# Three convolution slots, an attention bank for the value chunk, and conv loads a block ahead, in a hybrid encoder kernel

## The chip, the core and the metric

The kernel runs on one core of a Trainium2 chip. The core has five engines with instruction streams of their own: TensorE (PE, matmuls and transposes; its weight loads are listed as PEld), VectorE (DVE), ScalarE (ACT), GpSimd (POOL) and SyncE (SP). In this kernel SyncE does nothing but issue transfers between HBM and the core's memory, in the order of its stream: one that has to wait holds up those behind it. Matmuls write into banks of PSUM, all other tiles live in SBUF. The metric is device time in microseconds (us): 1510.81 is the median of three runs (1509.77 to 1511.25).

## What is computed

One encoder layer, applied to a prompt of 512 tokens and to a sample of 1024 tokens, with 1024 channels and in float32:

```python
h = _rmsnorm(x, norm_attn_g[l])
z = h @ w_in[l]            # q | k | v | ca | cb
a_out = _window_attn(q, k, v, bias, band, attn_sink[l])
c = ca * jax.nn.sigmoid(cb)
c = _dwconv(c, conv_dw_w[l], conv_dw_b[l])            # 31 taps
c = jax.nn.silu(_layernorm(c, conv_ln_g[l], conv_ln_b[l]))
x = x + jnp.concatenate([a_out, c], axis=-1) @ w_out[l]
h = _rmsnorm(x, norm_ffn_g[l])
u = _dwconv(h @ w_up[l], ffn_dw_w[l], ffn_dw_b[l])    # 3 taps
x = x + (jax.nn.silu(u[..., :D_FF]) * u[..., D_FF:]) @ w_down[l]
y = _rmsnorm(x, norm_final_g)
```

## The kernel before

**Products.** Every large product is made of three matmuls: both factors are split into a rounded part ("hi") and the rest ("lo"), and hi x hi, hi x lo and lo x hi are added in PSUM. So each chunk of weights is loaded raw, cast to its hi part by ScalarE (L225) and subtracted to its lo part by GpSimd or VectorE (L226). The three matmuls stand on lines 337, 338 and 340 for the projections, and on 761, 762 and 763 for the out-projection.

**Memory.** `Slots` (L70) hands out fixed slots of SBUF by class: 15 q slots of 4096 bytes, 4 c slots of 4224, 61 h slots of 2048, 2 d slots of 2176 and 32 small ones (L188). A tile takes the smallest class that fits, in the order in which slots were given back. A name like h14_260_1700 is slot h14, its 260th tile, the 1700th of the program. PSUM's eight banks are dealt out in the same way: three a, two u, two b and one c; the table `use` says which a job may take (L190). In the sample's pass the projections (job "step") may take b alone, the attention (job "attn") a or u.

**Stages.** 0 to 105 us: norm and projection of the prompt. 105 to 320: the projection of the sample by chunks of w_in, in two halves of 512 tokens (`step`, L483, which calls `evac`, L407, to take a finished chunk from its bank); beside it, as side work, the attention and out-projection of the prompt. 340 to 650: the up-projection of the prompt (`ffn_step`), with the attention of the sample beside it (`sample`). 650 to 755: the out-projection of the sample, block by block (the loop at L1141), with three kinds of side work: the right halves of w_out (`right_halves`), the layer norms of the convolution's blocks (`conv_norm`, L713) and eleven sums of pairs (`pair_sums`, L923). Behind that the up-products and down-products of the sample, with an order on PE that is written by hand.

**What the change touches.** In `evac`, the value chunk (the last branch, from L448 on) is copied from its bank by ScalarE (L450), transposed by four PE instructions into a second bank (L453), and split from there (L460, L461). `conv_norm(i)` loads block i of the convolution from DRAM (cvd, L719) and its half of the concatenation (L711), transposes it on PE (L725), normalises (L731 on VectorE), transposes back (L737) and applies the swish. `pair_sums(p)` loads 512 KB from DRAM (gt[p]) into a c slot g (L926), makes four sums on GpSimd into a second c slot r (L932 to L935) and stores r to gb[p] (L936). gt[p] was stored by the gated steps of the prompt (L921), the last one being gt10.

**What sets the order.** `tick` (L315) advances side work: after each group of matmuls a rate is added to `due`, and for each whole unit one step of a generator runs. All instructions then pass a scheduler, which orders each engine's stream by priorities and modelled times; slots and banks are bound to tiles in program order. A transfer into a slot waits until the slot's last reader is done, and where that reader is a store, until it has landed.

Of the kernel before, what the change touches and what calls it, by code (L numbers as in the profile page):

```python
# [15 lines left out]
P = 128  # L16
# [35 lines left out]
NE = 2  # L52
# [5 lines left out]
KEEP = 3  # L58
# [111 lines left out]
def tile_hybrid_encoder(ctx: ExitStack, tc: tile.TileContext, xs, rel_bias, norm_attn_g, w_in,  # L170
                        attn_sink, conv_dw_w, conv_dw_b, conv_ln_g, conv_ln_b, w_out, norm_ffn_g,
                        w_up, ffn_dw_w, ffn_dw_b, w_down, norm_final_g, onehot, outs):
    nc = tc.nc
# [9 lines left out]

    homes = dict(q=full, h=big, c=odd, d=odd, s=small)
    small.tile([P, FILL], F32, name="fill")
    for tag, n in (("d0", 576), ("d1", 576), ("c0", 1088), ("c1", 1088), ("c2", 1088), ("c3", 1088)):
        odd.tile([P, n], F32, tag=tag, name=f"{tag}_0", bufs=1)
    sb = Slots(lambda tag: homes[tag[0]], dict(q=(15, 4096), c=(4, 4224), h=(61, 2048), d=(2, 2176), s=(32, 64)), "q", KEEP)  # L188
    banks = Slots(lambda tag: ps[two_of[tag]], dict(a=(3, 2048), u=(2, 2048), b=(2, 2048), c=(1, 2048)))
    use = dict(step="aub", turn="aub", last="c", conv="c", attn="au", norm="b", out="b", up="u", down="b")  # L190

# [3 lines left out]
    def bank(job):  # L195
        return banks.tile([NT], among=use[job])
# [210 lines left out]
    def evac(kind, c, nt, src):  # L407
        g, n = (0, 0) if nt == 0 else (1, nt - 1)
        T = GR[g]["T"]
        cols = slice(n * NT, (n + 1) * NT)  # L410
        if kind == "cb":
            t = sb.tile([NT])
            nc.scalar.activation(t[:], src, AF.Tanh, scale=0.5)
            tanh_t[nt, c] = t
        elif kind == "ca":
            if n == 0:
                cp = sb.tile([T + 2 * PAD])
                nc.gpsimd.memset(cp[:, 0:PAD], 0.0)
                nc.gpsimd.memset(cp[:, PAD + T:2 * PAD + T], 0.0)
                cpads[g, c] = cp  # L420
            cp = cpads[g, c]
            nc.vector.scalar_tensor_tensor(cp[:, PAD + n * NT:PAD + (n + 1) * NT], tanh_t.pop((nt, c))[:], 1.0, src,
                                           op0=ALU.add, op1=ALU.mult)
        elif kind == "q":
            hi, lo = sb.tile([NT], F32R), sb.tile([NT], F32R)
            nc.scalar.activation(hi[:], src, AF.Identity, scale=QSCALE)
            nc.vector.scalar_tensor_tensor(lo[:], src, QSCALE, hi[:].bitcast(F32),
                                           op0=ALU.mult, op1=ALU.subtract)
            for e in range(2):
                for L, s in ((0, hi), (1, lo)):  # L430
                    nc.sync.dma_start(
                        qsd[nt][:, L * HD:(L + 1) * HD, 2 * c + e, :].rearrange("b p t -> p b t"),
                        s[e * HD:(e + 1) * HD, :].bitcast(F32).rearrange("p (b t) -> p b t", t=P))
        elif kind == "k":
            hi, lo = sb.tile([NT], F32R), sb.tile([NT], F32R)
            nc.scalar.copy(hi[:], src)
            nc.vector.tensor_tensor(lo[:], src, hi[:].bitcast(F32), op=ALU.subtract)
            for kv in range(NKV):
                if g == 0:
                    kt[0, kv] = [sb.tile([T], F32R) for _ in range(2)]  # L440
                for L, s in ((0, hi), (1, lo)):
                    src_k = s[kv * HD:(kv + 1) * HD, :].bitcast(F32)
                    if g == 0:
                        for half in range(2):
                            nc.sync.dma_start(kt[0, kv][L][half * HD:(half + 1) * HD, :].bitcast(F32), src_k)
                    else:
                        nc.sync.dma_start(ksd[:, kv, L, cols], src_k)
        else:  # L448
            vs = sb.tile([NT])
            nc.scalar.copy(vs[:], src)  # L450
            pt = bank("step")
            for i in range(4):
                nc.tensor.transpose(pt[:, i * P:(i + 1) * P], vs[:, i * P:(i + 1) * P], ident[:])  # L453
            src = pt[:].rearrange("p (b c) -> p b c", c=P)
            vs = []
            for kv in range(NKV):
                v = sb.tile([4, P], F32R)
                head = slice(kv * HD, (kv + 1) * HD)
                rest = slice((1 - kv) * HD, (2 - kv) * HD)
                nc.scalar.copy(v[:, :, head], src[:, :, head])  # L460
                nc.vector.tensor_tensor(v[:, :, rest], src[:, :, head], v[:, :, head].bitcast(F32), op=ALU.subtract)  # L461
                if g == 1:
                    nc.sync.dma_start(vsd[:, n, kv], v[:].bitcast(F32))
                vs.append(v)
            if g == 0:
                vt[0] = vs
# [241 lines left out]
    def load_cat(i):  # L708
        cats[i, 0] = (sb.tile([4, P], F32R), sb.tile([4, P], F32R))
        for L in range(2):  # L710
            nc.sync.dma_start(cats[i, 0][L][:].bitcast(F32), catd[blocks[i][1], :, L, :].rearrange("p (j t) -> p j t", t=P))  # L711

    def conv_norm(i):  # L713
        G, b = blocks[i]
        if G["g"] == 0:
            drain(convs)
        cat = cat_of(i, 1)
        cv = sb.tile([4, P])
        nc.sync.dma_start(cv[:], cvd[G["g"]][:, :, b * P:(b + 1) * P])  # L719
        if G["g"] == 1 and (i, 0) not in cats:  # L720
            load_cat(i)
        yield 0.0
        pt = bank("norm")
        for c in range(4):
            nc.tensor.transpose(pt[:, c * P:(c + 1) * P], cv[:, c, :], ident[:])  # L725
        st, mv, rs = sm(6), sm(2), sm(1)
        nc.vector.bn_stats(st[:], pt[:])
        nc.vector.bn_aggr(mv[:], st[:])
        rstd_of(mv[:, 1:2], 1.0, rs[:])
        xh = sb.tile([CCH])  # L730
        nc.vector.tensor_scalar(xh[:], pt[:], mv[:, 0:1], rs[:], op0=ALU.subtract, op1=ALU.mult)  # L731
        del pt
        for _ in range(YN):
            yield 0.0
        p2 = bank("norm")
        for c in range(4):
            nc.tensor.transpose(p2[:, c * P:(c + 1) * P], xh[:, c * P:(c + 1) * P], ident[:])  # L737
# [215 lines left out]
    def sample():  # L953
# [13 lines left out]
        drain(late)  # L967
        for m in range(NE):
            yield from conv_norm(4 + m)
        for kc in range(KC):  # L970
            load_wo(kc, 1)

# [164 lines left out]

    side.extend((right_halves(), conv_norm(4 + NE)))
    side.extend(pair_sums(p) for p in range(NPAIR))
    pace.update(rate=2.2)  # L1140
    for i in range(4, NB - 2):  # L1141
        if 4 < i < NB - NE:
            side.appendleft(conv_norm(i + NE))
        if i == 8:
# [569 lines left out]
```

## Time and profile before

| what | value |
|---|---|
| median of three runs | 1510.81 us |
| the profiled execution | 1509.34 us, span 1507.5 us |
| mean granted clock of PE | 0.997 |
| PE busy | 1484.8 us, 98% of the span |
| PE's waits in the first 110 us | 3.1 us (L274, L296, L337, L338) |
| PE's waits behind 750 us | 2.7 us (L1119 on ACT, L1121 on POOL, L1042 on DVE) |

In the page and the views, one row is one instruction or a group. "a<-h,h" says which kind of slot or bank is written from which. "[1.92 <-DMA h<-qsd]" is idle time of the engine ahead of the row, and what ended it. Matmuls overlap in the array, so that their listed time (0.39 us) is longer than the step from one start to the next. SPq rows are issues of transfers; when one landed is read from the engine that waited for it.

### The profile page before, as it was taken

To read this page: it belongs to the slowest core of one execution; us is meant where nothing else is said; L and a number is where in the kernel's file an instruction comes from. 1 tells how busy PE (TensorE), PEld (TensorE's weight loads), DVE (VectorE), ACT (ScalarE), POOL (GpSimd) and SP (SyncE) were. 2 spreads that over 40 slices of the span, in tenths; PEclk is the share of its full clock that TensorE was granted. 3 is DMA by queue.
4 is the path that set the end of the run, shared out by engine and by line. 5 is a ranking of instruction groups with operands and counts; after the bars stand their busy time and mean duration, and the time that the engine had idled before them with its cause. 6 is when DMAs were issued, how large, how long until landed. Compare 5 with 4: busy or idle time off the path is not lost. (4 is left out here: it accounts for less than half of the span.)

```text
span 1507.5 us, 20010 instructions
## 1 busy us (share of the span) xinstructions
PE 1484.8 (98%) x6857; PEld 1225.2 (81%) x6857; DVE 1125.6 (75%) x1612; ACT 801.9 (53%) x1417; POOL 686.6 (46%) x546
## 2 busy tenths in 40 slices
PE   9999999999999999999999999999999999999998
PEld 7888787888888888778877888888888888888886
DVE  4889888878698885756868777777776845568884
ACT  6635646435877777534355554454445633444254
POOL 6642435236766676665325554554554000003345
PEclk9999999999999999999999999999999999999999
DMA  7762335455444436796222333333331772356644
GB/s 231 219 194 69 105 98 147 140 175 177 145 133 126 134 123 200 247 343 227 89 71 92 100 100 100 105 105 106 105 119 64 235 266 84 109 171 222 218 165 168
DMA packets 222443, 227.16 MB, mean 151 GB/s; under 512 B 12564, under 2 KB 162012, under 8 KB 222213
## 3 DMA queue, kind: packets, MB, share of 16 engines
q1 hardware_dynamic: 222341, 225.88, 46.6%
q8 instruction: 54, 0.88, 0.2%
q14 instruction: 48, 0.39, 0.1%
HBM read 164.74 MB, written 62.14 MB: 150 GB/s over the span
## 5 line engine op out<-in xcount | busy, mean ns | idle before, releaser
L226 POOL TENSOR_TENSOR q<-q,q 128x1024 fp32r<-128x1024 f32 x72 | 174.2, 2423 | 100.4 <-ACT q L225 37.2
L995 POOL TENSOR_TENSOR q<-q,q 128x512 fp32r<-128x512 f32 x101 | 140.8, 1401 | 154.0 <-ACT q L1105 141.8
L995 DVE TENSOR_TENSOR h<-h,h 128x512 fp32r<-128x512 f32 (+2 forms) x202 | 154.5, 797 | 67.1 <-ACT h L999 26.6
L1461 PE MATMUL w<-h,h 128*128 128x512 f32 x462 | 179.7, 389 | 0.0
L1459 PE MATMUL w<-h,h 128*128 128x512 f32 x458 | 178.2, 389 | 0.0
L1460 PE MATMUL w<-h,h 128*128 128x512 f32 x458 | 178.2, 389 | 0.0
L1119 PE MATMUL w<-h,q 128*128 128x512 f32 x448 | 175.0, 391 | 1.4 <-ACT w L1199 1.4
L1121 PE MATMUL w<-h,q 128*128 128x512 f32 x448 | 174.4, 389 | 1.1 <-POOL q L995 1.1
L1120 PE MATMUL w<-h,q 128*128 128x512 f32 x426 | 165.8, 389 | 0.0
L337 PE MATMUL u<-h,q 128*128 128x512 f32 x384 | 153.3, 400 | 1.6 <-DVE h L889 1.2
L338 PE MATMUL u<-h,q 128*128 128x512 f32 x384 | 151.4, 394 | 0.3 <-DVE h L299 0.3
L340 PE MATMUL u<-h,q 128*128 128x512 f32 x368 | 144.3, 392 | 0.0
L392 DVE SCALAR_TENSOR_TENSOR c<-c,cvw,c 128x512 f32<-128x512 f32 x184 | 138.1, 751 | 2.6
L992 POOL TENSOR_TENSOR q<-q,q 128x1024 f32<-128x1024 f32 x12 | 32.7, 2738 | 230.7 <-DVE q L992 213.4
L999 ACT CAST h<-h 128x512 fp32r<-128x512 f32 x120 | 72.0, 620 | 92.1 <-DVE h L995 40.6
L225 ACT CAST q<-q 128x1024 fp32r<-128x1024 f32 (+1 forms) x73 | 75.8, 1044 | 60.4 <-POOL q L226 23.4
L337 PE MATMUL b<-h,q 128*128 128x512 f32 x264 | 105.3, 400 | 0.0
L338 PE MATMUL b<-h,q 128*128 128x512 f32 x264 | 104.5, 396 | 0.0
L340 PE MATMUL b<-h,q 128*128 128x512 f32 x264 | 104.1, 395 | 0.3 <-POOL q L226 0.3
L1461 PEld LDWEIGHTS w<-h,h 128*128 128x128 f32 x462 | 86.7, 188 | 18.0
L1459 PEld LDWEIGHTS w<-h,h 128*128 128x128 f32 x458 | 86.0, 188 | 18.0
L1119 PEld LDWEIGHTS w<-h,q 128*128 128x128 f32 x448 | 84.2, 188 | 20.1 <-ACT w L1199 2.6
(435 smaller groups left out, 3657.7 us busy)
## 6 DMA issues: line engine op xcount, KB each, us to landing
q<-in_w_up SPq DMA_DIRECT2D x88, 512.0 KB
ga<-q SPq DMA_DIRECT2D x64, 256.0 KB
h<-ga SPq DMA_DIRECT2D x57, 256.0 KB
q<-in_w_in SPq DMA_DIRECT2D x28, 512.0 KB
h<-in_w_down SPq DMA_DIRECT2D x52, 256.0 KB
q<-in_x_sample SPq DMA_DIRECT2D x15, 512.0 KB
x1d<-q SPq DMA_DIRECT2D x11, 512.0 KB
gt<-h SPq DMA_DIRECT2D x22, 256.0 KB
```

What stands on the lines that cost most here:

```text
L226: ins = (nc.vector if dve else nc.gpsimd).tensor_tensor(lo[:], raw[:], hi[:].bitcast(F32), op=ALU.subtract)
L337: nc.tensor.matmul(out, whi[:, kc, :], hi[:], start=(kc == 0), stop=False)
L338: nc.tensor.matmul(out, whi[:, kc, :], lo[:], start=False, stop=False)
L340: nc.tensor.matmul(out, wlo[:, kc, :], hi[:], start=False, stop=(kc == KC - 1))
L392: nc.vector.scalar_tensor_tensor(acc[:], src(t), w(t), acc[:], op0=ALU.mult, op1=ALU.add)
L995: (eng or nc.vector).tensor_tensor(out, a, b, op=ALU.subtract)
L1119: nc.tensor.matmul(out, whi[:, s], hi[:], start=(start and c == 0), stop=False, **go)
L1120: nc.tensor.matmul(out, whi[:, s], lo[:], start=False, stop=False, **go)
L1121: nc.tensor.matmul(out, wlo[:, s], hi[:], start=False, stop=(stop and c == 3), **go)
L1459: nc.tensor.matmul(out, sh[:, c], th[:], start=(p == 0), stop=False)
L1460: nc.tensor.matmul(out, sh[:, c], tl[:], start=False, stop=False)
L1461: nc.tensor.matmul(out, sl[:, c], th[:], start=False, stop=(p == NPAIR - 1))
```

## The change

It has four parts.

1. One c slot fewer and two h slots more (L186 to L188): 3 x 4224 + 63 x 2048 = 141,696 bytes in place of 4 x 4224 + 61 x 2048 = 141,824.
2. In the sample's pass the value chunk's transposes take a bank of the attention, a or u, and no longer one of the two b banks (L451).
3. The load of a convolution block is taken out of `conv_norm` into `load_conv`, and the loop over the blocks calls it a block ahead; the first such load is issued at the end of `sample`.
4. The rate of side work in the out-projection's first blocks is 1.5 in place of 2.2.

```diff
-    for tag, n in (("d0", 576), ("d1", 576), ("c0", 1088), ("c1", 1088), ("c2", 1088), ("c3", 1088)):
+    for tag, n in (("d0", 576), ("d1", 576), ("c0", 1088), ("c1", 1088), ("c2", 1088)):
...
-    sb = Slots(..., dict(q=(15, 4096), c=(4, 4224), h=(61, 2048), d=(2, 2176), s=(32, 64)), "q", KEEP)
+    sb = Slots(..., dict(q=(15, 4096), c=(3, 4224), h=(63, 2048), d=(2, 2176), s=(32, 64)), "q", KEEP)
...
-            pt = bank("step")
+            pt = bank("attn" if g else "step")
...
+    cvs = {}
+
+    def load_conv(i):
+        G, b = blocks[i]
+        cv = cvs[i] = sb.tile([4, P])
+        nc.sync.dma_start(cv[:], cvd[G["g"]][:, :, b * P:(b + 1) * P])
+        if G["g"] == 1 and (i, 0) not in cats:
+            load_cat(i)
+
     def conv_norm(i):
...
-        cv = sb.tile([4, P])
-        nc.sync.dma_start(cv[:], cvd[G["g"]][:, :, b * P:(b + 1) * P])
-        if G["g"] == 1 and (i, 0) not in cats:
-            load_cat(i)
-        yield 0.0
+        if i not in cvs:
+            load_conv(i)
+            yield 0.0
+        cv = cvs.pop(i)
...
             yield from conv_norm(4 + m)
+        load_conv(4 + NE)
...
-    pace.update(rate=2.2)
+    pace.update(rate=1.5)
     for i in range(4, NB - 2):
+        if i + NE + 1 < NB:
+            load_conv(i + NE + 1)
```

NE is 2 and NB is 12. The number of instructions is the same on every engine (PE 6858, DVE 1614, ACT 1275, SP 783, POOL 551); what moves is the order, and the slots and banks. Lines behind 710 are numbered 8 to 11 higher in the new program.

**First place: PE at the value chunk, about 153 to 160 us before.** L453 is the transposes of the value chunk, L666 and L610, L680 and L681 the prompt's attention, L337 to L340 the projection; h14_260 and h10_261 are queries loaded from DRAM. Before:

```order
L453 MATMUL b1_88_1686<-ident_91,h8_258_1684 128x128 [waits DVE_49,Activation_49]
L453 MATMUL b1_88_1686<-ident_91,h8_258_1684 128x128 x3
...
L681 MATMUL a2_85_1616<-q14_248_1598,h34_145_867 128x512 [waits DVE_49]
L680 MATMUL a2_85_1616<-q14_248_1598,h34_145_867 128x512
...
L610 MATMUL u0_102_1866<-h1_127_767,h14_260_1700 128x384 [waits DMAHW7_49,DVE_49]
L610 MATMUL u0_102_1866<-h2_128_768,h14_260_1700 128x384
L337 MATMUL b1_91_1713<-h4_130_781,q9_234_1493 128x512 [waits DVE_49,PE_49]
L338 MATMUL b1_91_1713<-h22_131_782,q9_234_1493 128x512
L340 MATMUL b1_91_1713<-h4_130_781,q1_235_1494 128x512
```

Now the transposes stand amid the projection into b1_91, in bank a0, and a cluster of attention comes later, ahead of the first lo matmul into b0_109:

```order
L337 MATMUL b1_91_1714<-h35_148_881,q4_235_1493 128x512
L453 MATMUL a0_88_1685<-ident_90,h18_258_1683 128x128 [waits Activation_49]
L453 MATMUL a0_88_1685<-ident_90,h18_258_1683 128x128 x3
L338 MATMUL b1_91_1714<-h31_149_882,q4_235_1493 128x512
...
L338 MATMUL b0_109_1948<-h38_84_553,q6_273_1798 128x512
L680 MATMUL u0_98_1795<-q0_205_1275,h33_146_869 128x512 [waits Activation_49]
L681 MATMUL u0_98_1795<-q7_269_1757,h33_146_869 128x512 [waits DVE_49]
...
L666 MATMUL u0_106_1917<-ident_90,h9_264_1707 128x128 [waits DVE_49,PE_49]
...
L680 MATMUL a1_108_1941<-q9_289_1916,h32_145_866 128x512 [waits Activation_49]
L340 MATMUL b0_109_1948<-h37_83_552,q10_274_1799 128x512 [waits Pool_49]
```

That L340 waits for POOL, where the subtraction that writes q10_274 (L226, from the raw chunk q3_253) now stands behind the one that writes q1_295 and behind an L692 of the attention, which waits for VectorE's L690 (h15_279). POOL now:

```order
L692 TENSOR_TENSOR q8_247_1591<-h15_257_1672,h16_256_1671 64x512 [waits DVE_49]
L645 TENSOR_SCALAR q11_266_1724<-q11_266_1724,s5_263_1703 128x384 [waits DVE_49,PE_49]
L226 TENSOR_TENSOR q1_295_1945<-q12_272_1796,q14_294_1944 128x1024 [waits DMAHW2_49,Activation_49]
L692 TENSOR_TENSOR q8_247_1591<-h15_279_1842,h16_278_1841 64x512 [waits DVE_49,Pool_49]
L226 TENSOR_TENSOR q10_274_1799<-q3_253_1640,q6_273_1798 128x1024 [waits DMAHW6_49,Pool_49]
```

Before, the same subtraction (it wrote q4_273 there) stood ahead of both.

**Second place: PE at the prompt's last scores, about 247 to 254 us before.** L666 transposes weights of the attention, L680 and L681 use the copies of these transposes; the last L340 takes a chunk's lo part. Before:

```order
L666 MATMUL u0_144_2606<-ident_91,h18_350_2394 128x128
L338 MATMUL b1_142_2579<-h56_155_910,q14_348_2375 128x512
...
L338 MATMUL b0_146_2653<-h38_84_554,q11_364_2509 128x512
L680 MATMUL a2_145_2614<-h8_374_2595,h35_146_870 128x512 [waits DVE_49,Activation_49]
L681 MATMUL a2_145_2614<-q3_375_2596,h35_146_870 128x512 [waits DVE_49]
L680 MATMUL a2_145_2614<-q3_375_2596,h35_146_870 128x512 [waits Activation_49]
L681 MATMUL a2_145_2614<-q4_376_2611,h35_146_870 128x512 [waits DVE_49]
L340 MATMUL b0_146_2653<-h37_83_553,q12_365_2510 128x512 [waits Pool_49]
```

Now (the last L666 into u0_143 stands 30 rows ahead of the L680 shown, and the last two scores, of q14_378, 25 rows behind it):

```order
L338 MATMUL b0_146_2655<-h38_84_553,q7_366_2510 128x512
L680 MATMUL a1_145_2615<-h18_376_2596,h33_146_869 128x512 [waits DVE_49,Activation_49]
L733 MATMUL u1_147_2682<-ident_90,h14_387_2674 128x128 x3
L681 MATMUL a1_145_2615<-h5_377_2597,h33_146_869 128x512 [waits DVE_49]
L340 MATMUL b0_146_2655<-h37_83_552,q2_367_2511 128x512 [waits Pool_49]
L337 MATMUL b0_146_2655<-h39_85_568,q7_366_2510 128x512
```

**Third place: SP in the out-projection, from about 650 us before.** gt is loaded into g, r is stored to gb; cvd and catd are loads for the layer norms. Before, a load takes c0 or c2, a store c1 or c3:

```order
L936 DMA gb3_3448<-c3_1090_6928 128x1024 [waits DMAHW3_49,Pool_49]
L926 DMA c2_1108_7030<-gt5_3439 128x1024 [waits DMAHW5_49]
L214 DMA q4_1161_7325<-in_x_sample 128x1024 [waits PE_49]
L921 DMA gt10_3444<-h33_1025_6582 128x512 [waits DMAHW6_49,Pool_49]
L719 DMA h0_1080_6880<-cvd1_168 128x4x128 [waits DMAHW7_49,PE_49]
L711 DMA h15_1081_6882<-catd_166 128x512 [waits DMAHW0_49,PE_49]
L936 DMA gb4_3449<-c1_1107_7009 128x1024 [waits DMAHW1_49,Pool_49]
L926 DMA c0_1110_7050<-gt6_3440 128x1024 [waits DMAHW2_49]
```

Now c0, c1 and c2 go round, and a load into a slot follows the store out of the same slot (gb2 out of c0, then gt4 into c0; gb3 out of c2, then gt5 into c2; gb4 out of c1, then gt6 into c1):

```order
L944 DMA gb2_3450<-c0_1110_7009 128x1024 [waits DMAHW3_49,Pool_49]
L711 DMA h5_1048_6699<-catd_165 128x512 [waits DMAHW4_49,DVE_49]
L214 DMA q5_1138_7179<-in_x_sample 128x1024 [waits PE_49]
L934 DMA c0_1128_7123<-gt4_3441 128x1024 [waits DMAHW3_49]
...
L944 DMA gb3_3451<-c2_1112_7036 128x1024 [waits DMAHW0_49,Pool_49]
...
L934 DMA c2_1130_7150<-gt5_3442 128x1024 [waits DMAHW6_49,DMAHW0_49]
L944 DMA gb4_3452<-c1_1129_7124 128x1024 [waits Pool_49]
...
L718 DMA h38_1097_6943<-cvd1_167 128x4x128 [waits DMAHW3_49,DVE_49]
L934 DMA c1_1174_7421<-gt6_3443 128x1024 [waits DMAHW7_49,DMAHW4_49]
L929 DMA gt10_3447<-h8_1045_6690 128x512 [waits DMAHW5_49,Pool_49]
```

The last row is the store of the last gated step; the cast that takes the slot h8 next (h8_1057, from a raw part of w_out's right half) comes behind it on ScalarE, and PE's first out-projection matmul with that cast behind the cast.

More of the change, by code (lines that the diff above doesn't have):

```diff
@@ L185, in tile_hybrid_encoder @@
     small.tile([P, FILL], F32, name="fill")
-    for tag, n in (("d0", 576), ("d1", 576), ("c0", 1088), ("c1", 1088), ("c2", 1088), ("c3", 1088)):
+    for tag, n in (("d0", 576), ("d1", 576), ("c0", 1088), ("c1", 1088), ("c2", 1088)):
         odd.tile([P, n], F32, tag=tag, name=f"{tag}_0", bufs=1)
-    sb = Slots(lambda tag: homes[tag[0]], dict(q=(15, 4096), c=(4, 4224), h=(61, 2048), d=(2, 2176), s=(32, 64)), "q", KEEP)
+    sb = Slots(lambda tag: homes[tag[0]], dict(q=(15, 4096), c=(3, 4224), h=(63, 2048), d=(2, 2176), s=(32, 64)), "q", KEEP)
     banks = Slots(lambda tag: ps[two_of[tag]], dict(a=(3, 2048), u=(2, 2048), b=(2, 2048), c=(1, 2048)))
```

## The prediction

> **What bounds the kernel now.** I read the page from the top, then the waits of TensorE, then stretches of time, then single rows. The page first (busy time, share of the span, instructions):
>
> ```profile
> span 1507.5 us, 20010 instructions
> ...
> PE 1484.8 (98%) x6857; PEld 1225.2 (81%) x6857; DVE 1125.6 (75%) x1612; ACT 801.9 (53%) x1417; POOL 686.6 (46%) x546
> ```
>
> TensorE (PE) is the bound, and its matmuls are not touched by the change: both programs have 6858 PE instructions. So the change can only win time in which PE waits, or runs below its clock, and can only lose time by new waits. The profiled execution took 1509.34 us, 1.84 more than its span and 1.47 below the median of 1510.81; I work out differences against it and apply them to the median.
>
> How much waiting is there? The view of PE's waits over the whole span (engine, line, written tile, what ended the wait, us, times, longest), the rows that bear on the change:
>
> ```profile
> PE u L610 <- DMA h<-qsd: 1.9, 1, 1.9
> ...
> PE u L337 <- DVE h L889: 1.2, 1, 1.2
> PE a L725 <- DMA h<-cvd: 1.1, 1, 1.1
> ...
> PE b L453 <- ACT h L450: 0.8, 1, 0.8
> ...
> PE c L761 <- DVE q L766: 0.6, 1, 0.6
> PE u L761 <- ACT h L225: 0.5, 1, 0.5
> ...
> PE a L737 <- DVE h L731: 0.4, 1, 0.4
> ```
>
> These seven come to 6.5 us, 0.4% of the time. The same in stretches (length, PE busy and count, weight loads, DVE, ACT, POOL, granted clock, DMA share, GB/s):
>
> ```profile
> 150.00:160.00 10.00, 6.69 (x38) 5.01 (x37) 9.00 (x21) 9.03 (x21) 2.02 (x2) 1.00 0.49 158
> 160.00:170.00 10.00, 10.00 (x44) 8.30 (x44) 7.31 (x17) 4.66 (x12) 4.65 (x4) 0.83 0.09 30
> ...
> 250.00:260.00 10.00, 8.54 (x34) 5.89 (x33) 7.17 (x8) 9.14 (x17) 8.94 (x5) 1.00 0.96 274
> ...
> 650.00:660.00 10.00, 9.77 (x44) 7.79 (x43) 4.56 (x6) 3.22 (x6) 7.61 (x11) 1.00 0.83 275
> 660.00:670.00 10.00, 8.33 (x38) 6.32 (x37) 4.26 (x7) 0.62 (x1) 6.23 (x8) 1.00 1.06 388
> 670.00:680.00 10.00, 9.17 (x42) 6.93 (x41) 4.39 (x9) 2.76 (x6) 7.39 (x13) 1.00 1.06 395
> ```
>
> Three places lose time where the change moves rows: the value chunk of the sample's projection (150 to 165 us), the prompt attention beside it (250 to 256), and the sample's out-projection (650 to 680). Behind 760 us the order on PE is the same in both programs, so I count that part at nothing.
>
> **The value chunk (line 451).** PE's timeline (start, us, what it is, and in brackets the idle time before it):
>
> ```profile
> 145.05 0.39 PE L337 MATMUL b<-h,q 128*128 128x512 f32 x1
> ...
> 156.04 0.50 PE L681 MATMUL a<-q,h 128*128 128x512 f32 x1 [0.60 <-DVE q L669]
> ...
> 159.75 0.59 PE L610 MATMUL u<-h,h 128*128 128x384 f32 x2 [1.92 <-DMA h<-qsd]
> ...
> 161.09 0.61 PE L338 MATMUL b<-h,q 128*128 128x512 f32 x1
> ...
> 164.49 0.41 PE L337 MATMUL b<-h,q 128*128 128x512 f32 x1
> 164.74 0.39 PE L338 MATMUL b<-h,q 128*128 128x512 f32 x1
> 164.97 0.39 PE L340 MATMUL b<-h,q 128*128 128x512 f32 x1
> ```
>
> Matmuls of 512 columns start 0.23 us apart (164.74, 164.97), whatever their listed length. The waits of this place are 0.8 (L453) + 0.6 + 1.9 = 3.3 us. Behind them eight matmuls start from 161.09 to 164.49, 0.425 apart: the half clock that the stretch 160 to 170 shows as 0.83. They cost 3.40 - 8 x 0.23 = 1.6 us. Together **4.9 us**. The cause stands in the order: the transposes of the value chunk sit in one of the two b banks, the other holds the value itself, and pass 2 projects into b banks only, so PE has nothing but attention until they are read. With the transposes in an a bank the next projection follows at once. This wait goes.
>
> What is late next? In the new order the attention rows that were hidden come as a cluster later, and the first matmul that needs the low part of the convolution chunk behind them (L340 into b0_109) waits for a GpSimd subtraction that now stands behind L692, which waits for VectorE. What VectorE does here, grouped from 143 to 183 us, and POOL's two rows:
>
> ```profile
> L392 DVE SCALAR_TENSOR_TENSOR c<-d,cvw,c 128x512 f32<-128x512 f32 x26 | 19.5, 750 | 0.2
> L617 DVE CUSTOM_DVE_ANT_0 q<-u,h,nsink 128x384 f32<-128x384 f32 x4 | 2.5, 612 | 0.2 <-PE u L610 0.2
> L669 DVE TENSOR_TENSOR h<-u,h 128x512 fp32r<-128x512 f32 x3 | 2.1, 684 | 0.4 <-PE a L680 0.4
> ...
> L461 DVE TENSOR_TENSOR q<-b,q 128x256 fp32r<-128x256 f32 x3 | 1.3, 417 | 0.0
> ```
> ```profile
> 163.02 1.27 POOL L692 TENSOR_TENSOR q<-h,h 64x512 fp32r<-64x512 f32 x1 [10.90 <-DVE h L690]
> ...
> 169.13 2.42 POOL L226 TENSOR_TENSOR q<-q,q 128x1024 fp32r<-128x1024 f32 x1 [1.50 <-ACT q L643]
> ```
>
> In the new order VectorE does, from the key chunk's L437 (at about 146 us, as much work stands ahead of it as in the old order) to that L690: 24 L392 at 0.75, 9 L617 at 0.61, 9 of the L669 and L437 and L690 kinds at 0.68, 4 L461 at 0.42 and six small ones, some 32 us, of which about half a microsecond goes in rows that overlap. So L690 ends near 177.7, L692 (1.27) and the subtraction (2.42) near 181.4. PE gets there by its own work: the b0_87 matmul of 145.05 stands 1.2 us earlier in the new order, and from it to that L340 lie 115 matmuls of 512 columns, 18 of 384, 4 of 256 and 40 transposes, 34.1 us at their start-to-start times (0.227, and 0.175, 0.119 and 0.109 read the same way): 177.9. **New wait 3.5 us**; between 0 (if VectorE is not full) and 5.1 (if the half clock comes back with it). Net here -1.4, between -4.9 and +0.2.
>
> On that upper end the Trainium skill speaks too ("TensorE: Matmul & The Clock Gate", What's actually happening): after an idle window of about 3.4 us the array runs at half rate, until it was busy for as long. The trace agrees with 0.425 against 0.227 for 3.4 us, though the idle time before was 0.6 and 1.92 in pieces. By that rule the new wait brings the half clock again, and the value chunk gives nothing.
>
> **Prompt attention, 250 to 256 us.** The stretch 250 to 260 has 8.54 of 10 us busy:
>
> ```profile
> 250.37 0.40 PE L338 MATMUL b<-h,q 128*128 128x512 f32 x1
> ...
> 254.12 0.50 PE L340 MATMUL b<-h,q 128*128 128x512 f32 x1 [0.33 <-POOL q L226]
> ```
>
> Five steps take 3.75 us where 5 x 0.23 would be 1.15: 2.6 us, in L680 and L681, which wait for the copies of transposes that stand only eight rows ahead. In the new order those transposes stand about 30 rows ahead, and the last pair of scores is 25 rows further on. Nothing in the diff aims at it; the scheduler gives it. I take **-2.0**, between -2.6 and 0, since the L340 still waits for a GpSimd subtraction.
>
> **The out-projection (lines 186 to 188, load_conv, pace).** The loads of the convolution's blocks, issued a block ahead, end the L725 wait (1.1) and the L737 wait (0.4). Of L337's 1.2 and L761's 0.6, which hang on VectorE, I take half: 0.9. The L761 behind ScalarE (0.5) is the other side of the change. Its rows, of SyncE's queue (the start is the issue of a transfer), of POOL, of ScalarE and of PE:
>
> ```profile
> 380.21 0.32 SPq L926 DMA_DIRECT2D c<-gt  x1
> ...
> 635.78 0.32 SPq L936 DMA_DIRECT2D gb<-c  x1
> ...
> 651.30 0.38 SPq L926 DMA_DIRECT2D c<-gt  x1
> ...
> 664.86 1.02 SPq L926 DMA_DIRECT2D c<-gt  x1
> ...
> 669.12 0.57 SPq L921 DMA_DIRECT2D gt<-h  x1
> ```
> ```profile
> 383.50 0.74 POOL L933 TENSOR_TENSOR c<-c 128x256 f32<-128x256 f32 x1 [2.46 <-DMA c<-gt]
> ...
> 655.83 0.74 POOL L932 TENSOR_TENSOR c<-c 128x256 f32<-128x256 f32 x1 [1.76 <-DMA c<-gt]
> ...
> 672.16 0.73 POOL L932 TENSOR_TENSOR c<-c 128x256 f32<-128x256 f32 x1 [1.32 <-DMA c<-gt]
> ```
> ```profile
> 675.08 0.62 ACT L225 CAST h<-h 128x512 fp32r<-128x512 f32 x1 [5.57 <-DMA gt<-h]
> ```
> ```profile
> 675.75 0.50 PE L761 MATMUL u<-h,h 128*128 128x512 f32 x1 [0.46 <-ACT h L225]
> ```
>
> A pair sum loads 512 KB into one c slot (g), adds into another (r) and stores r. With four slots, loads use c0 and c2 and never wait for a store. With three, **every load from the third pair on takes the slot of an earlier store and waits on SyncE's queue until that store has landed**; all that is queued behind it waits too. Behind it stands the last gt store, whose slot the last cast of w_out's right half overwrites, and PE needs that cast. New path from the first store: store, load, four sums of 0.73, store, load, four sums, store, gt store, cast. With d for one transfer that is 6 d + 5.8 + 0.6 + about 1.7 for issue = 6 d + 8.1. The first store was issued at 635.78; earlier gains (1.4 + 2.0) and half of L337's bring it to 631.8. So the cast ends at 639.9 + 6 d. PE gets to its matmul at 675.75 - 2.3 (ten matmuls fewer stand ahead) - 3.4 (earlier gains) - 2.5 (waits of this stage that go) = 667.5. Break-even d = 4.6 us. The trace gives d from both sides: 3.29 unloaded (380.21 to 383.50), 4.53 (651.30 to 655.83), 5.96 (669.12 to 675.08), 7.30 (664.86 to 672.16, in stretches of 388 to 395 GB/s). The new order has fewer transfers in flight, so I take 4.9, nearest to the 4.53 row: cast at 669.3, **wait 1.8 us**. Net here: -2.5 - 0.4 + 1.8 = **-1.1**; with d = 3.3 it is -2.9, with 6.2 it is +6.7.
>
> [...]
>
> The other edits: two more 2 KB slots and one 4.2 KB slot fewer (141,824 bytes become 141,696) change which slot is reused; the fourth convolution input into the old slot of the first comes 57 VectorE rows after its last reader, so no wait. The pace of 1.5 for 2.2 spreads side work; what it hides behind are 0.23 us matmuls that are there anyway. Nothing for either; if the cover fails, it shows as one more wait of the 0.4 to 1.2 us kind listed above.
>
> Sum: -1.4 - 2.0 - 1.1 = **-4.5 us**, 1504.8 for the profiled execution, **1506.3** on the median.
>
> **Rivals.**
> *Three slots make it slower.* One mechanism, one place: the cast behind the gt store. At d = 6.2, the middle of the loaded rows above (4.53 to 7.30), the cast ends at 677.1, PE waits 9.6 us, the total is +3.3: 1514.1. It decides from d = 6.1 on. For it: DMA is 83 to 106% busy there. Against it: the waiting itself empties the queues.
> *The wait only moves.* The new wait at b0_109 brings the half clock with it (+1.6), or d is 5.2 to 6.1: total -3 to +3, for instance 1507.9. For it: VectorE is 9.00 of 10 us busy in 150 to 160.
> *All goes, nothing comes.* d near 3.3 and a VectorE that is not full: -1.8 more in the out-projection, -3.5 more at the value chunk, total -9.8: 1501.0. For it: the unloaded row, and idle VectorE time in 160 to 170 (7.31 of 10).
>
> **How the numbers follow.** About 3 us, 0.2%, is what a measurement of this kernel can tell from none. Forecast (1503.5 to 1507.8): 0.38. All goes: 0.12. Wait only moves: 0.29. Slower: 0.21. So faster 0.50, same 0.29, slower 0.21. The range for 8 in 10 goes from a little below the full gain to d = 6.3: 1500 to 1515.
>
> **What would show it.** In the changed profile: no L453 wait and no load wait near 155 us (step 1 right); a PE wait near 178 to 182 us for POOL's L226 or for VectorE, and a granted clock below 1 behind it or not; five score steps near 250 us under 2 us in all; no wait on cvd loads; one wait near 667 us of PE on ScalarE's cast, whose length against 1.8 gives d. Wrong would be: PE waits elsewhere before 760 us, where the scheduler moved rows that I did not follow, or waits behind 760 us, where other slots are reused.

## The result, and the profile after

The changed kernel takes **1546.07 us** (median of four runs, 1542.47 to 1548.09) against 1510.29 (1508.52 to 1511.25) for the kernel before on the same chip: ratio 1.0242, 95% interval 1.0229 to 1.0254. It is slower by 36 us, far outside the predicted 1500 to 1515. The profiled execution took 1544.78 us, 35.4 more than that of before. The page of the changed kernel (span; busy time, share, instructions):

```profile
span 1543.0 us, 19950 instructions
...
PE 1493.6 (97%) x6857; PEld 1229.0 (80%) x6857; DVE 1129.0 (73%) x1612; ACT 799.6 (52%) x1417; POOL 694.1 (45%) x546
```

PE has the same matmuls and stays the bound; the new time must be waits and half clock. PE's waits over the whole span after (engine, line, written tile, releaser, us, times, longest):

```profile
PE w L1128 <- DVE q L1257: 13.4, 7, 3.5
PE w L1128 <- ACT w L1210: 8.2, 11, 1.2
PE u L337 <- DVE h L897: 4.6, 2, 3.4
PE u L769 <- issue: 4.0, 1, 4.0
...
PE a L610 <- DVE h L669: 1.2, 1, 1.2
PE u L666 <- DVE h L690: 1.1, 1, 1.1
...
PE a L680 <- ACT q L668: 0.7, 1, 0.7
```

The two largest stand in the part that the prediction counted at nothing: L1128 is the first of the three matmuls of an up-product, L1257 ends the three-tap convolution (`dwconv`) that reads a wide bank, L1210 copies a first product into a bank. Before, the first does not occur and the second comes to 1.4 us in three pieces. Two of the waits (3.48 us ending at 967, 2.99 ending at 1092) have half clock with them as well (granted clock 0.84 in 960 to 970, 0.83 in 1090 to 1100).

Both programs have the same number of PE rows, so lost time can be compared by row: the start of a row, less the start-to-start times at full clock (0.227, 0.175, 0.119 and 0.109 us by size) of the rows ahead of it.

| PE rows (start before, us) | what stands there | lost before | lost after | difference | predicted |
|---|---|---|---|---|---|
| to 900 (192) | start, value chunk | | | +2.0 | -1.4 |
| 900 to 1350 (290) | prompt attention | 4.7 | 0.5 | -4.2 | -2.0 |
| 1350 to 1800 (386) | first up-product of the prompt | 0.6 | 5.7 | +5.1 | 0 |
| 1800 to 3000 (634) | up-projection of the prompt | 3.4 | 3.6 | +0.2 | 0 |
| 3000 to 3900 (827) | out-projection | 8.4 | 13.3 | +4.8 | -1.1 |
| 3900 to 5400 (1170) | up-products of the sample | 1.8 | 29.3 | +27.5 | 0 |
| behind | down-products | -0.4 | -0.4 | 0 | 0 |

The differences come to 35.4 us, the whole of it (the base of the first stretch is arbitrary, so that only its difference stands; 0.6 of its 2.0 come before the value chunk). The up-products by stretch, before and after (length, PE busy and count, weight loads, DVE, ACT, POOL, granted clock, DMA share, GB/s); first before:

```profile
850.00:1150.00 300.00, 298.64 (x1315) 246.40 (x1314) 223.48 (x216) 147.64 (x217) 157.47 (x109) 1.00 0.31 103
```

and after, with the stretches that answer to those of the prediction:

```profile
160.00:170.00 10.00, 10.00 (x51) 8.45 (x50) 9.93 (x23) 5.69 (x15) 3.84 (x3) 1.00 0.32 105
...
180.00:190.00 10.00, 8.16 (x23) 5.98 (x24) 4.09 (x7) 5.64 (x12) 7.53 (x5) 0.66 0.10 32
250.00:260.00 10.00, 10.00 (x47) 8.19 (x47) 7.15 (x10) 6.88 (x14) 4.50 (x5) 1.00 0.82 230
350.00:360.00 10.00, 6.63 (x29) 5.15 (x28) 4.79 (x8) 4.70 (x6) 4.98 (x4) 0.96 0.90 279
...
660.00:670.00 10.00, 6.05 (x15) 4.79 (x16) 8.13 (x12) 2.85 (x5) 3.44 (x5) 0.66 0.96 311
```
```profile
850.00:1150.00 300.00, 278.57 (x1196) 224.95 (x1196) 206.36 (x197) 134.66 (x198) 144.03 (x99) 0.99 0.29 93
```

In 300 us PE did 119 matmuls fewer; at 0.228 us (300 / 1315) that is 27 us. All other engines did less too, so none of them became the bound: the engines wait for one another.

**Where the chain starts.** The value half's conv reads a wide bank (w3 here) once the sum in it is complete, and PE needs the bank back. Before, VectorE and then ScalarE:

```profile
884.43 0.70 DVE L992 TENSOR_TENSOR w<-w,h 128x512 f32<-128x512 f32 x1 [0.20 <-PE w L1121]
```
```profile
885.16 1.21 ACT L1244 ACTIVATE c<-w,vecs,fw 128x1024 f32<-128x1024 f32 x1
```

The sum ends at 885.13 and the conv starts at 885.16. The same step after, on VectorE, ScalarE and PE:

```profile
897.80 0.70 DVE L1001 TENSOR_TENSOR w<-w,h 128x512 f32<-128x512 f32 x1 [0.20 <-PE w L1130]
...
907.62 1.28 DVE L1257 SCALAR_TENSOR_TENSOR q<-w,fw,q 128x1023 f32<-128x1023 f32 x1
```
```profile
903.73 1.21 ACT L1255 ACTIVATE q<-w,vecs,fw 128x1024 f32<-128x1024 f32 x1
...
908.99 0.57 ACT L1210 COPY w<-w 128x512 f32<-128x512 f32 x1 [2.41 <-DVE q L1257]
```
```profile
909.62 0.50 PE L1128 MATMUL w<-h,q 128*128 128x512 f32 x1 [0.97 <-ACT w L1210]
```

The sum ends at 898.50, the conv starts at 903.73: 5.2 us late. It writes a q slot where it wrote a c slot. Which one, the program's rows say (a tile is slot, number in the slot's class, number in the program):

```
before  ACT  L1244 ACTIVATE c2_1342_8867<-w3_12_8600
after   PE   L1130 MATMUL w1_14_8741<-h36_1234_7880,q5_1335_8755      (starts at 902.82)
after   ACT  L1255 ACTIVATE q5_1347_8871<-w3_12_8604                  (starts at 903.73)
```

The slot's last tenant, q5_1335, holds the operands of product 6, twelve matmuls of which the last starts at 902.82. The conv cannot write there before, and the scheduler has put it on ScalarE behind that. From late conv to late bank is one chain: conv, L1257, L1210, PE. The other half of the loss hangs on it too. The late conv makes the sums of the pair (x, e, y) late, these are stored to ga late, and the gate's conv of the next step writes over e, whose store is the third of four. From the pair ahead of the one above, SyncE (issue of the stores of x twice, then e), ScalarE and PE after:

```profile
868.37 2.01 SPq L1291 DMA_DIRECT2D ga<-q  x2
...
871.27 0.56 SPq L1291 DMA_DIRECT2D ga<-q  x1
```
```profile
876.32 1.21 ACT L1255 ACTIVATE q<-w,vecs,fw 128x1024 f32<-128x1024 f32 x1 [2.22 <-DMA ga<-q]
```
```profile
882.98 0.47 PE L1128 MATMUL w<-h,q 128*128 128x512 f32 x1 [2.50 <-DVE q L1257]
```

That the slot hand-overs alone are the cause had to be tested: the engines' orders differ as well, and other parts of the change could have moved them.

### The profile page after: what moved, and what is told of

Its sections match the earlier page's. It is cut to its first block, busy times and chain, and to the rows that moved or that the text cites. A ratio compares the mean times of both kernels' runs of the same rounds, so it can differ in the third digit from the quotient of the medians.

```text
span 1543.0 us, 19950 instructions
## 1 busy us (share of the span) xinstructions
PE 1493.6 (97%) x6857; PEld 1229.0 (80%) x6857; DVE 1129.0 (73%) x1612; ACT 799.6 (52%) x1417; POOL 694.1 (45%) x546
## 5 line engine op out<-in xcount | busy, mean ns | idle before, releaser
L1004 POOL TENSOR_TENSOR q<-q,q 128x512 fp32r<-128x512 f32 x110 | 165.5, 1510 | 196.8 <-ACT q L1114 178.7
L226 POOL TENSOR_TENSOR q<-q,q 128x1024 fp32r<-128x1024 f32 x72 | 174.4, 2428 | 134.9 <-ACT q L225 52.0
L1128 PE MATMUL w<-h,q 128*128 128x512 f32 x506 | 200.4, 396 | 21.7 <-DVE q L1257 13.4
L1004 DVE TENSOR_TENSOR h<-h,h 128x512 fp32r<-128x512 f32 (+1 forms) x206 | 155.9, 792 | 63.2 <-ACT h L1008 25.6
L1130 PE MATMUL w<-h,q 128*128 128x512 f32 x506 | 198.1, 392 | 0.7 <-POOL q L1004 0.7
L1129 PE MATMUL w<-h,q 128*128 128x512 f32 x484 | 189.6, 392 | 0.0
L337 PE MATMUL u<-h,q 128*128 128x512 f32 x384 | 154.0, 401 | 5.0 <-DVE h L897 4.6
L340 PE MATMUL u<-h,q 128*128 128x512 f32 x368 | 144.8, 394 | 0.0
L1128 PEld LDWEIGHTS w<-h,q 128*128 128x128 f32 x506 | 95.7, 189 | 48.9 <-issue 16.2
L1130 PEld LDWEIGHTS w<-h,q 128*128 128x128 f32 x506 | 95.7, 189 | 21.3 <-POOL q L1004 1.1
L1129 PEld LDWEIGHTS w<-h,q 128*128 128x128 f32 x484 | 91.6, 189 | 18.4
L337 PE MATMUL b<-h,q 128*128 128x512 f32 x264 | 106.2, 402 | 0.0
L340 PE MATMUL b<-h,q 128*128 128x512 f32 x264 | 104.6, 397 | 0.0
```

Of the source, the lines that this page charges most:

```text
L226: ins = (nc.vector if dve else nc.gpsimd).tensor_tensor(lo[:], raw[:], hi[:].bitcast(F32), op=ALU.subtract)
L337: nc.tensor.matmul(out, whi[:, kc, :], hi[:], start=(kc == 0), stop=False)
L340: nc.tensor.matmul(out, wlo[:, kc, :], hi[:], start=False, stop=(kc == KC - 1))
L1004: (eng or nc.vector).tensor_tensor(out, a, b, op=ALU.subtract)
L1128: nc.tensor.matmul(out, whi[:, s], hi[:], start=(start and c == 0), stop=False, **go)
L1129: nc.tensor.matmul(out, whi[:, s], lo[:], start=False, stop=False, **go)
```

## Experiments

Ratios are to the kernel before on the same chip, with 95% intervals; the unit is us. The expectations name theories. A: one big slot (q or c) fewer, 18 for 19, starves the up-products. N, later: the number of slots in any class. F: the gate's conv over the slot of e, whose store is the last one issued. G: the value half's conv over the slot that a product has just read.

**e1, the slots back.** The change with lines 186 and 188 as before.

> The changed kernel with the slots of before (four of 4.2 KB, 61 of 2 KB); the value chunk's bank, the loads a block ahead and the pace stay changed. Theory A (one big slot fewer makes the loss: 27 us in the up-products, where a tile of the gate's convolution has to wait for a slot, and about 4 us in the out-projection, where pair sums wait for a store): the up-products lose under 4 us again, the wait of 4 us near 660 us goes, and the time is 1505 to 1512. Rival B (the moved order makes the loss, whichever slots there are): 1535 to 1548, with waits on VectorE's L1257 in the up-products as in the changed kernel.

Measured 1508.91 (1506.38 to 1512.74), ratio 0.9993, 0.9981 to 1.0006. Without the slots nothing is lost on balance.

**e2, the slots alone.**

```diff
-for tag, n in (..., ("c2", 1088), ("c3", 1088)):
+for tag, n in (..., ("c2", 1088)):
-dict(q=(15, 4096), c=(4, 4224), h=(61, 2048), ...)
+dict(q=(15, 4096), c=(3, 4224), h=(63, 2048), ...)
```

> The kernel before with three slots of 4.2 KB and 63 of 2 KB, and nothing else changed. Theory A: slower by 27 us in the up-products and by 3 to 8 us ahead of them, 1538 to 1548. Rival B: 1508 to 1513. Rival C (the slots and the new order do it only together): between, 1515 to 1535.

Measured 1540.14, ratio 1.0195, 1.0179 to 1.0210: the slots by themselves make most of the loss, 27.3 us of it by row in the up-products. PE's waits there are those of the change, somewhat shorter (line numbers are 9 to 11 lower):

```profile
PE w L1119 <- DVE q L1246: 11.1, 7, 2.3
PE w L1119 <- ACT w L1199: 7.0, 10, 1.2
```

**e6, the big slot given back in another class.** The change, with `q=(16, 4096), c=(3, 4224), h=(61, 2048)`: 19 big slots as before.

> The changed kernel with 61 slots of 2 KB and 16 of 4 KB in place of 63 and 15, still three of 4.2 KB: again 19 big slots, but the pair sums still go round in three. Theory A splits its loss here: the up-products' 27 us go, the wait near 660 us (4 us, with a half-clock stretch of 1.6 behind it) stays; 1513 to 1521. Rival D (it is the number of 4.2 KB slots that counts in the up-products, not the number of big ones): 1538 to 1548. Rival B: 1535 to 1548.

Measured 1534.36, ratio 1.0167, 1.0124 to 1.0210. Most of the loss stays with 19 big slots (21.3 us by row in the up-products), against theory A.

**e7, four slots until the up-products, three from there on.** The kernel before, and a tile that is never used, taken as the up-products begin:

```diff
+    held_back = sb.tile([2, NT], among="c")
     for guard in reversed(ps_guards):
```

> The kernel before, with one of its four 4.2 KB slots taken out of use from the up-products on; all before that is the same. Theory A: the up-products lose 25 to 30 us by waits of PE on VectorE's last reading of a wide bank, every second step; 1533 to 1542. Rival B and rival E (the two more 2 KB slots change which slot is reused, and that does it): 1509 to 1513.

Measured 1513.36, ratio 1.0023, 1.0014 to 1.0032: 3 us slower, not the 25 to 30 of theory A. With 18 big slots in the up-products and three of them c, 5.6 us are lost there by row, against 1.8 before and 29.3 in the change. Theory A falls as the cause of the large loss: it is not how many slots there are, but which tile comes into which. From step 2 to step 17 of the 22 (0 to 21), the value half's conv takes a q slot in every second step in e2, e6 and the change; before, and in e1 and e7, it finds a c slot in all of them.

**e8 and e9, the order of giving back.** One line at the end of `value_part`, in the changed kernel (e8) and in the kernel before (e9). With it the gate's next conv takes another tile's slot: x for e in e8, e for x in e9.

```diff
         for i, b in ((5, x[:, R]), (7, x[:, L]), (6, e[:, R]), (3, y[:])):
             nc.sync.dma_start(ga[i, p][:], b)
+        del t, x, e
```

> The change whole (three big slots, 63 of 2 KB); only the order in which value_part's last tiles are given back is turned from t, e, x to t, x, e, so that the gate's dwconv of the next step takes the slot of x (whose stores to ga 5 and 7 are issued before) and not that of e (whose store to ga 6 is issued last). Theory F (which of the stored tiles dwconv writes over): the 2.2 us waits of ScalarE's L1255 for the ga store, 14.4 us in seven, shrink to under half, PE's waits for a wide bank fall from 21.6 us in 18 to under 8, and of the 27.4 us lost in the up-products 18 to 27 come back: 1519 to 1528 us. Theory N (the number of big or 2 KB slots): nothing of it comes back, 1543 to 1549 us.

> The kernel before with its four big slots and nothing else of the change; only the same order of giving back is turned, t, x, e. There dwconv takes the slot of x as it stands, and takes that of e after this edit, with the split's copy on that of x. Theory F: the loss of the change appears without any of its slots: PE waits for VectorE's L1246 and ScalarE's L1199 by 15 to 22 us, and the time is 1528 to 1540 us. Theory N: the time of before, 1508 to 1513 us.

e8: 1532.91, ratio 1.0141, 1.0121 to 1.0162; 13 us of the 36 came back, between what the theories gave. e9: 1508.95, ratio 0.9989, 0.9978 to 1.0001: no loss. So F is not the cause as it stood: with e's slot under the gate's conv the kernel before loses nothing, since its stores are early. F is a second link, and works only where the stores are late already. PE's waits between 770 and 1160 us in e8:

```profile
PE w L1128 <- ACT w L1210: 10.1, 10, 3.1
...
PE w L1128 <- DVE q L1257: 1.7, 1, 1.7
```

The wait behind the stores has gone from 13.4 to 1.7, that behind L1210 has stayed: what makes it lies ahead of both.

**e3, e5, e12: the other parts.** e3 is the kernel before with `pt = bank("attn" if g else "step")` alone, e5 with `rate=1.5` alone, e12 with e3's edit and the change's `load_conv` (e12 and `rate=1.5` make e1).

> The kernel before with the value chunk's transposes in a bank of their own kind alone. PE's wait of 4.9 us near 181 us goes, and the chunk of 100 to 200 us gains 2 to 4 us of PE busy time (the three edits without the slots showed 99.58 us busy there against 96.69). If what is gained there is kept to the end: 1506 to 1508 us. If the out-projection, where the DMA engines are busy over 0.9, waits it off again between 640 and 690 us: 1509 to 1512 us, with PE's waits there larger by 2 to 4 us.

> The kernel before with the pace of side work in the out-projection at 1.5 for 2.2 alone. The three edits without the slots had one wait of PE of 5.0 us at 666.9 us, for ScalarE's cast of a right half of the output weights. If the slower pace makes it (side work that casts those halves and sums the pairs is drawn later): a wait of 3 to 6 us for that cast here too, and 1511 to 1515 us. If the earlier arrival of PE or the layer norm's loads make it: no wait of over 1.5 us for the cast, and 1508 to 1512 us.

> The kernel before with the value chunk's bank and the earlier layer norm loads, four big slots, the pace left at 2.2. The bank alone gave 1504.3 us; all three without the slots 1508.9 us, with one wait of 5.0 us for the cast of a right half of the output weights at 667 us. If the earlier loads make that wait (they stand ahead of the output weights on SP while the DMA engines are full): the wait is here too, 4 us or more, and 1506 to 1511 us. If the slower pace makes it, with PE early: no such wait, and PE's wait of 1.5 us for the layer norm's load (L725) goes: 1501.5 to 1504.5 us.

e3: **1504.27** (1502.25 to 1509.57), ratio 0.9961, 0.9948 to 0.9974, faster than both kernels and better than expected. e5: 1511.85, 1.0007, 0.9998 to 1.0016, nothing that can be told from zero, and no wait of over 1.1 us for the cast. e12: 1509.82, 0.9992, 0.9978 to 1.0006: with the loads a block ahead, most of what the bank gave is gone (the intervals of e3 and e12 do not overlap). The out-projection from 640 to 700 us, in e3 and in e12:

```profile
640.00:700.00 60.00, 56.79 (x264) 45.50 (x264) 33.82 (x45) 20.70 (x43) 40.99 (x55) 1.00 0.90 314
```
```profile
640.00:700.00 60.00, 54.42 (x245) 44.32 (x244) 35.98 (x50) 24.49 (x50) 39.12 (x52) 0.94 0.95 333
```

With the early loads PE does 19 matmuls fewer. The expectation had asked about a wait for the cast; PE waits for the layer norm instead: 3.4 us for VectorE's L739 and 1.8 for a cvd load, which now stands a block ahead and still lands late, at a DMA share of 0.95. By row the out-projection lost 11.6 us in e12, against 9.0 in e3 and 8.4 before. That is 2.6 of the 5 or so that the medians differ by; this one profile does not place the rest, since it has 5.3 us more at the value chunk as well, which e1, with the same order on PE there, does not have.

**e10 and e11, the slot of the value half's conv.** The changed kernel, three big slots and all; e11 has e8's line too.

```diff
-    def dwconv(src, f):
+    def dwconv(src, f, among=None):
-        u = sb.tile([W2])
+        u = sb.tile([W2], among=among)
-        uv = dwconv(s.pop("wy"), NJ + j)
+        uv = dwconv(s.pop("wy"), NJ + j, "c")
```

> The change whole; only the value half's dwconv takes its 4 KB tile from the class of the three big slots in every step (as it does in the kernel before), where the change gives it, in every second step, the slot that the operands of product 6 held, which TensorE has just read. The order in which t, e and x are given back is left. Theory G (a conv tile in a slot whose last reader is the product just before comes late, and so does the wide bank that it frees): PE's waits for a wide bank fall from 21.6 us in 18 to under 10 and 12 to 24 us come back: 1522 to 1534 us. If the gate's conv over e's slot is the whole cause: nothing, 1543 to 1549 us.

> The change whole, with both edits of the slots' order: the value half's dwconv in a big slot, and t, x, e given back in this order so that the gate's dwconv takes x's slot. Still three big slots and 63 of 2 KB. Theory G with F (each of the two slot hand-overs costs its part, and nothing else in the up-products does): PE's waits between 770 and 1160 us are under 5 us, as before the change, and the 27 us are back: 1515 to 1522 us, what is left being the wait at 359 us and the out-projection. Theory N (the number of slots costs something there by itself): 1525 us or more.

e10: 1515.13, ratio 1.0033, 1.0020 to 1.0046; e11: 1514.63, 1.0027, 1.0013 to 1.0041. One slot for another gives back 31 us of 36, more than expected (27.6 us by row in the up-products), and e8's line adds nothing on top of it. The edit is narrow: from the value half's conv of step 0 to that of step 17, the programs of e10 and of the change put 27 of 272 tiles into different slots, the 18 of this conv (ten from q to c, eight from one c slot to another) and nine tiles of operands that move from c1 to c2. e10, PE's waits between 770 and 1160 us, then VectorE and ScalarE (the sum in the bank, the conv), then the stretch:

```profile
PE w L1128 <- ACT w L1210: 1.6, 2, 1.1
```
```profile
852.73 0.70 DVE L1001 TENSOR_TENSOR w<-w,h 128x512 f32<-128x512 f32 x1 [0.20 <-PE w L1130]
```
```profile
853.47 1.21 ACT L1255 ACTIVATE c<-w,vecs,fw 128x1024 f32<-128x1024 f32 x1
```
```profile
850.00:1150.00 300.00, 298.90 (x1319) 247.13 (x1319) 224.95 (x219) 151.95 (x220) 161.78 (x110) 1.00 0.32 104
```

The conv starts 0.04 us after its bank is ready, the stretch has 1319 matmuls where before had 1315, and of the seven waits for ga that L1255 had between 850 and 1150 us none is left, although e is still under the gate's conv. G is the cause, and F hung on it.

**e13, the slots with this mended, and the bank.** The kernel before with e2's, e3's and e10's edits.

> The kernel before with three big slots and 63 of 2 KB, the value chunk's bank, and the value half's dwconv held to the big slots; loads of the layer norm and pace as before. The bank alone gave 1504.3 us. If the slots, with their one bad hand-over mended, bring the 2 us of the prompt's attention and cost only the wait at 359 us (2.7 to 3.4 us and 1.6 us of half clock): 1504 to 1508 us. If they also make the out-projection's wait for L769 (2.3 to 4.0 us in the runs with the whole change): 1508 to 1513 us.

Measured 1514.23, ratio 1.0025, 1.0016 to 1.0034: slower than either expectation. The up-products are whole (300.00 of 300 us busy between 850 and 1150), so the slots (three c, 63 h) cost some 10 us against e3 ahead of them. By stretch, first e3, then e13:

```profile
170.00:200.00 30.00, 30.00 (x149) 25.07 (x148) 28.36 (x55) 21.71 (x44) 19.50 (x15) 1.00 0.29 92
240.00:260.00 20.00, 18.24 (x84) 14.29 (x84) 14.41 (x14) 14.68 (x27) 15.62 (x9) 1.00 0.77 224
350.00:370.00 20.00, 20.00 (x97) 16.93 (x96) 19.83 (x50) 11.71 (x27) 11.21 (x7) 1.00 0.29 85
```
```profile
170.00:200.00 30.00, 26.45 (x116) 21.53 (x115) 20.89 (x44) 18.93 (x39) 19.13 (x13) 0.89 0.31 97
240.00:260.00 20.00, 20.00 (x97) 16.48 (x96) 15.96 (x25) 13.42 (x26) 12.21 (x12) 1.00 0.69 193
350.00:370.00 20.00, 16.55 (x67) 13.23 (x67) 14.12 (x32) 10.56 (x19) 11.43 (x6) 0.91 0.53 163
```

At 0.228 us each, 33 matmuls (7.5 us) are lost at the value chunk, 13 (3.0) won at the prompt's attention and 30 (6.8) lost at 359. All three go with the slots: e10 has them too (112, 98 and 71 matmuls). By row another 2.8 us are lost in the out-projection (11.8 against 9.0). Why the value chunk's wait comes with these slots was not followed; e6, with three c slots and one more q, does not have it (148).

## Why the prediction was wrong

**The step that failed** is "Behind 760 us the order on PE is the same in both programs, so I count that part at nothing", with its companion in "the other edits" on the slots: "Nothing for either". PE's order is written by hand there, but ScalarE's, VectorE's and SyncE's are not, and a slot carries a dependence whatever PE's order is. The slots are handed out in order of return, so one slot less anywhere shifts which tile follows which in the whole rest of the program. Here the shift put the value half's conv on the operands of product 6: +27.5 us in the profile, where e10's three changed lines take back 27.6 (and 31 us of the whole by median). The prediction named the case ("waits behind 760 us, where other slots are reused") and gave it neither a price nor a chance.

**The value chunk.** That the wait of 4.9 us goes was right, and with the slots left alone (e3) nearly nothing came in its place: 0.4 us of waits between 140 and 200 us. By row 5.1 us are gained there, most of e3's 5.7 by median. In the change VectorE's L690 ended almost when predicted (178.8, said 177.7), but PE waited one cluster earlier than said, in the attention rows themselves, four times:

```profile
178.92 0.41 PE L666 MATMUL u<-ident,h 128*128 128x128 f32 x2 [1.10 <-DVE h L690]
179.93 0.47 PE L610 MATMUL u<-h,h 128*128 128x256 f32 x2 [0.38 <-PE u L666]
181.57 0.72 PE L610 MATMUL a<-h,h 128*128 128x256 f32 x2 [1.17 <-DVE h L669]
182.97 0.79 PE L680 MATMUL a<-q,h 128*128 128x512 f32 x1 [0.67 <-ACT q L668]
```

They come to 3.3 us (predicted 3.5). The L340 that was to wait for POOL has no wait of its own: it starts at 183.62, just behind its subtraction, which ended near 183.6 (said 181.4). The half clock came back too, and for twice as long as before: 0.66 in 180 to 190, where before had 0.83 in 160 to 170. So the chunk lost 1.3 us more than before, not 1.4 less, and more than the upper end of +0.2, which allowed 1.6 us for half clock: by row the rows 800 to 900 lost 7.2, 3.3 in waits and 3.9 beside them. That the size of the waits came out was in part luck, since other rows waited, for other releasers.

The prediction had weighed a rule of the Trainium skill ("TensorE: Matmul & The Clock Gate", What's actually happening), by which the half clock comes behind an idle window of about 3.4 us and the value chunk gives nothing. The half clock did come (0.66), though no single idle time here was longer than 1.2 us, and the chunk gave less than nothing.

**The prompt's attention** gave 4.2 us, not 2.0, in the direction predicted: the stretch 250 to 260 is full. It is the slots that give it, not the other edits: e3 has 84 matmuls in 240 to 260, e13 97.

**At 359 us** the prediction saw nothing. ScalarE before, then after:

```profile
352.79 2.00 ACT L225 CAST q<-q 128x1024 fp32r<-128x1024 f32 x2 [2.21 <-DMA q<-in_w_up]
354.70 0.77 ACT L893 ACTIVATE h<-u,vecs,fw 128x512 f32<-128x512 f32 x1
```
```profile
354.04 2.00 ACT L225 CAST q<-q 128x1024 fp32r<-128x1024 f32 x2 [5.71 <-DMA q<-in_w_up]
355.94 0.77 ACT L901 ACTIVATE h<-u,vecs,fw 128x512 f32<-128x512 f32 x1
```
```profile
358.96 0.57 PE L337 MATMUL u<-h,q 128*128 128x512 f32 x1 [3.37 <-DVE h L897]
```

The order is the same on ScalarE: two casts of fresh weights, then the conv that frees PE's bank. But PE came 2.2 us earlier (the gains ahead), and the weights landed 1.25 us later. Both became a wait of 3.4 us, and nine steps at half clock behind it (3.72 us from 358.96 to 362.68, where 2.04 would do) cost 1.7 more. A gain ahead of a transfer that does not come earlier is handed back there.

**The out-projection.** The chain was right, its exit was not. Loads do wait for the stores in their slots, and the first store (L944, issued at 638.59) and the end of the last cast (679.33) are 40.7 us apart, so that 6 d + 8.1 gives d = 5.4 where 4.9 was taken. But PE was stopped 15 us ahead of that cast, by rows that the prediction did not follow; POOL, VectorE and PE:

```profile
656.06 0.74 POOL L940 TENSOR_TENSOR c<-c 128x256 f32<-128x256 f32 x1 [4.09 <-issue]
...
658.14 1.29 POOL L928 TENSOR_TENSOR h<-h,h 128x512 f32<-128x512 f32 x1
```
```profile
659.47 1.21 DVE L226 TENSOR_TENSOR h<-h,h 128x512 fp32r<-128x512 f32 x1 [6.95 <-POOL h L928]
...
662.33 1.52 DVE L897 SCALAR_TENSOR_TENSOR h<-u,fw,h 128x511 f32<-128x511 f32 x2
```
```profile
663.95 0.77 PE L769 MATMUL u<-h,h 128*128 128x512 f32 x1 [4.03 <-issue]
```

The last gate product but one (L928; the last comes at 672.75) had its inputs at 650.4. On POOL it stands behind three of the sums of gt3, whose load was issued at 650.52 (SyncE had waited 3.8 us for a gt store to land and 0.8 for gb1's). VectorE's L226 needs a slot that L928 reads, and the conv that frees PE's bank stands behind it. The page puts PE's wait down to "issue"; its end is that of L897 at 663.85. Of the 2.5 us of waits that were to end, those for the cvd load and for VectorE's L766 did end, but L337's 1.2 stayed whole and the 0.4 behind the layer norm became 1.0; by e12 the early loads cost rather than give. In all +4.8 where -1.1 was predicted.

**The rivals.** "Three slots make it slower" had the sign and one of the stages, though not the row that stopped PE there, at a chance of 0.21 and a price of 1514.1; for over three quarters of the loss, the up-products, there was no rival. What stays open: why the value chunk's wait depends on the slots, and how the out-projection's loss divides. By row it lost 8.4 us before, 9.1 with the slots alone (e2), 12.8 with the other three edits alone (e1) and 13.3 with all; these are one profile each, and e13, with the slots and without the early loads, has 11.8.

## What to carry to other kernels

Where slots are handed out in order of return, a change of their number is a change of every hand-over behind it: list who follows whom in each slot that the inner loop uses, before and after, and ask for each pair whether the last reader is done when the new writer is due. A tile that frees the bottleneck's bank should have a slot of its own class; holding one such tile to it was worth 31 us here. Take the parts of a change singly, since the one that pays (0.4% here) can be hidden by the others.

## What was not expected of the hardware

In the change half clock followed the waits of 3.4 us at 359 and of 4.0 at 664, and also the one at 179 to 183 that came in four pieces of 0.4 to 1.2 us (3.3 together). In the up-products it came with single waits of 3.48 and 2.99 us, and not with the next longest, 2.50 us at 883. Behind the wait of 3.4 us at 359 it cost 1.7. And one execution can carry a wait of its own: e1 and e12 have the same rows on PE up to the out-projection, yet L337 waited 0.4 us for VectorE's L437 in the profile of the one and 2.9 in that of the other, at 155 us. A single profile places a wait; what it is worth takes the medians.
